# Silu and product of a block one step later, the third convolution tap issued apart, a gate block ahead of branch a

## The chip, the cores and the metric

The kernel runs on one core of a Trainium2 chip. It computes one layer of an encoder trunk on 512 tokens of width 2048, in fp32. The metric is the time of one execution in device microseconds (us), the median of several runs.

The engines in the tables: PE is TensorE (matmuls), PEld its weight loads, DVE is VectorE, ACT is ScalarE, POOL is GpSimd and SP is SyncE, which issues most of the DMAs. Each engine works off its own queue in order.

## The reference, cut to what matters

```python
h = rmsnorm(x, norm_mix[l])
proj = h @ w_in[l]
qa, ka, va, qb, kb, vb, ga, gb = jnp.split(proj, split_points, axis=-1)
...
merged = (jax.nn.sigmoid(ga) * (out_a @ w_branch_a[l])
          + jax.nn.sigmoid(gb) * (out_b @ w_branch_b[l]))
x = x + merged @ w_out[l]

h2 = rmsnorm(x, norm_ffn[l])
u = h2 @ w_up[l]
up = jnp.pad(u, ((0, 0), (1, 1), (0, 0)))
cw = conv_w[l]
u = up[:, :-2] * cw[0] + up[:, 1:-1] * cw[1] + up[:, 2:] * cw[2] + conv_b[l]
gate, val = jnp.split(u, 2, axis=-1)
x = x + (jax.nn.silu(gate) * val) @ w_down[l]
```

`out_a` is a windowed attention with 8 heads, `out_b` a neighbourhood attention with 8 heads. D_FF is 5632, so `w_up` has 11264 columns: 5632 for the gate and 5632 for the value.

## The kernel before

Activations lie transposed, 128 features on the partitions and 512 tokens along the row. Every fp32 product is made of three matmuls in the faster fp32r format: each operand is split into a rounded part (hi) and the rest (lo), the rounding by a cast on ACT and the rest by a subtraction on DVE, and hi·hi, hi·lo and lo·hi are added up in PSUM (L77). So every weight that PE uses passes through ACT and DVE first: L154 and L155 for most stages, L594 and L595 for the up-projection.

**Steps and units.** The layer is a list of steps: attention with its projections, then gate and branch blocks, w_out, 22 up-projection steps, and the down-projection. A step is a sequence of units; the weights of a unit are loaded by SP, split by ACT and DVE two units ahead of PE, and two buffers of each kind hold them, so the split for unit n+2 waits until PE has done unit n. After the matmuls of a unit were issued, `run_queued` takes entries from a queue of postponed work, in the up-projection one entry per unit. In an engine's queue that work stands among the splits in this order.

**Gates and branches.** A block is 512 output columns, four tiles m of 128 by 512. Before: gate blocks 0 and 1 of branch a, then `end_attention` (it closes the memory of attention and opens new pools, with all eight PSUM banks) and the loading and splitting of the eight `out_a` tiles through three scratch tiles (`split_out`), then the four blocks of branch a, then gate blocks 2 and 3. Where the gate came first, `evac_a` multiplies the matmul's result with it; where the branch came first, `evac_a` copies the result (L743) and `gate_after` multiplies later (L736).

**Up-projection.** A step makes 256 gate columns and 256 value columns with seven products in place of eight (a Strassen-like scheme): eight units (i = 0 to 7), each of 7 products with 2 halves with 3 matmuls of 256 columns, 42 in all. `Product.prep` (L594, L595) splits the seven combined weight blocks. Seven of the eight PSUM banks hold the sums; at the step's end `combine` reads them, first by the copy L673 on ACT, and the next step's matmuls take the banks as they come free. The results are two tiles with tag u, 128 by 1024 each: gate and val.

Then the work on them is put into the queue, and is done during the next step: scaling with the norm's row (`scale`, L832, DVE), the convolution over tokens (`conv`), Silu of the gate (L857, ACT), the product (L861, DVE) and the store to `act` in DRAM (L862, POOL). `conv` makes three scaled copies of a tile for the three taps, two ACT instructions each (L840, L842, L843), and adds the outer two to the middle one by two accumulating DMAs that POOL issues (L844, L845); the second waits for the first, as both write the same tile. Tag o (the sum) and tag a (the outer taps) have two buffers each. The queue of a step, by unit of the step in which it runs:

```python
wait, partial(scale, gate), pending_act.pop(),
lambda: held.update(g=conv(gate, 2 * s)), wait, partial(scale, val), silu,
lambda: held.update(v=conv(val, 44 + 2 * s))
```

The first entry runs at unit 7 of the step that made the tiles, the next ones at units 0 to 6 of the following step: scaling of the gate at 0, the product of the tiles of a step earlier at 1, convolution of the gate at 2, scaling of the value at 4, Silu at 5, convolution of the value at 6.

**Into and out of the up-projection.** The pool `w` for the split weights of the up-projection lies where the weight pool `wst` lay, and is opened in `post` of w_out's last block, after its matmuls and evacuations; then two products are split and the last two pairs of h2 formed (`form_pair`). During the last up step, `split_act` loads tiles of `act` back by SP and splits them (L890, L891) for the down-projection, load and split in one.

## Time and profile before

| | |
|---|---|
| median of 3 runs | 2581.73 us (2580.41 to 2588.13) |
| the profiled execution | 2588.31 us |
| its span, first to last instruction | 2586.5 us |
| mean granted clock of TensorE | 0.994 |
| up-projection, from the first to the last of its matmuls | about 1198 to 2104 us |

How to read it: the page gives, for each engine, the time in which it was busy and its share of the span. A list of waits gives who waited for whom, in total, how often and the longest. A timeline row gives start, duration, engine, line of the kernel, operation, output <- input and, in brackets, how long the engine had been idle before and what ended that. A windows row gives for a stretch of the span the busy time of each engine (with the number of instructions), the clock that PE was granted (1.00 is full), the share of the DMA engines that was busy, and what they moved in GB/s. A group row gives line, engine, operation, shapes, number, then busy time and the mean in ns of one, then idle time before them and what ended it. The ends of matmuls are modelled, so PE's idle time is a little rough.

### The profile page before, as it was taken

Reading aid. Unit: us, or ns where it says so; the run is one execution under the profiler, and the core shown is the slowest. Engines: PE = TensorE matmul, PEld = TensorE weight load, DVE = VectorE, ACT = ScalarE, POOL = GpSimd, SP = SyncE. Lnnn points to the kernel's source line nnn. Section 1 sums busy time; section 2 is a strip of 40 time slices with the busy share of each in tenths; the row PEclk is TensorE's granted clock in tenths of the full one; section 3 lists DMA queues with packets and bytes.
Section 4 is the critical chain, followed back from the end, with each engine's and each line's share of the span. In section 5 each row is a group of like instructions: output and inputs, shape, how many; then the busy total and the mean of one; then the engine's idle time right before and its main releaser. Section 6 shows DMA issues by size and latency. Waiting matters only on the chain.

```text
span 2586.5 us, 38229 instructions
## 1 busy us (share of the span) xinstructions
PE 2537.2 (98%) x15016; PEld 2254.9 (87%) x15016; DVE 1517.3 (59%) x2155; ACT 1123.6 (43%) x1617; POOL 206.4 (8%) x248
## 2 busy tenths in 40 slices
PE   9999999999999999999999999999999999999999
PEld 7888888888888888888999999999999988888887
DVE  6565554535454567656777787777778662242222
ACT  5355544432222233335555655566555562132111
POOL 0100000000000000100011111111111110000000
PEclk9999999999999999999999999999999999999999
DMA  5322232327777787854677877777777785464443
GB/s 184 98 83 90 87 96 92 96 90 269 239 260 251 250 278 270 286 188 155 165 200 186 214 198 193 215 192 198 188 185 202 214 252 169 134 214 136 130 126 111
DMA packets 294677, 464.67 MB, mean 180 GB/s; under 512 B 23136, under 2 KB 190688, under 8 KB 294496
## 3 DMA queue, kind: packets, MB, share of 16 engines
q1 hardware_dynamic: 249408, 348.00, 42.6%
q0 software_dynamic: 40480, 105.83, 16.6%
q10 hardware_dynamic: 4608, 8.39, 0.8%
q8 instruction: 117, 1.92, 0.3%
q14 instruction: 64, 0.52, 0.1%
HBM read 347.93 MB, written 68.16 MB: 161 GB/s over the span
## 4 chain that ended last, share of the span: by engine, by line
PE 88%; ACT 5%; DMA 4%; issue 2%; DVE 1%; SPq 0%; POOL 0%; ACTq 0%; POOLq 0%; DVEq 0%
PE mm L77 85%; DMA o<-a 3%; PE tr L77 2%; ACT wh L594 1%; ACT o L840 1%; ACT a L843 1%; ACT a L842 1%; PE tr L476 1%; PE tr L334 0%; DMA f<-in_w_up 0%; DVE wl L595 0%; ACT t L673 0%; DMA f<-sums 0%; DMA s<-act 0%; SPq L74 0%
## 5 line engine op out<-in xcount | busy, mean ns | idle before, releaser
L77 PE MATMUL mm<-s,hi 128*128 128x512 f32 x3712 | 1107.6, 390 | 3.9 <-ACT s L227 2.1
L77 PE MATMUL mm<-s,wh 128*128 128x256 f32 x4928 | 826.3, 281 | 33.6 <-ACT t L673 24.3
L77 PEld LDWEIGHTS mm<-s,hi 128*128 128x128 f32 x3712 | 696.7, 188 | 148.3 <-ACT s L227 2.5
L77 PEld LDWEIGHTS mm<-s,wh 128*128 128x128 f32 x4928 | 712.6, 190 | 38.5 <-ACT t L673 27.8
L155 DVE TENSOR_TENSOR lo<-raw,hi 128x1024 fp32r<-128x1024 f32 (+1 forms) x289 | 352.6, 1220 | 666.9 <-ACT hi L154 648.4
L77 PE MATMUL mm<-s,lo 128*128 128x512 f32 x1856 | 681.9, 390 | 0.0
L154 ACT CAST hi<-raw 128x1024 fp32r<-128x1024 f32 (+1 forms) x289 | 303.4, 1050 | 854.3 <-PE mm L77 792.8
L77 PE MATMUL mm<-s,wl 128*128 128x256 f32 x2464 | 589.9, 280 | 2.3 <-DVE wl L595 2.3
L595 DVE TENSOR_TENSOR wl<-f,wh 128x1024 fp32r<-128x1024 f32 x352 | 372.5, 1087 | 164.0 <-ACT wh L594 152.6
L594 ACT CAST wh<-f 128x1024 fp32r<-128x1024 f32 x352 | 315.2, 939 | 275.7 <-PE mm L77 211.5
L77 PEld LDWEIGHTS mm<-s,wl 128*128 128x128 f32 x2464 | 424.1, 190 | 2.9 <-DVE wl L595 2.9
L77 PEld LDWEIGHTS mm<-s,lo 128*128 128x128 f32 x1856 | 348.6, 188 | 71.5
L77 PE MATMUL mm<-hi,s 128*128 128x512 f32 x896 | 284.8, 394 | 5.7 <-ACT hi L154 5.7
L77 PEld LDWEIGHTS mm<-hi,s 128*128 128x128 f32 x896 | 167.7, 189 | 38.4 <-ACT hi L154 5.7
L77 PE MATMUL mm<-lo,s 128*128 128x512 f32 x448 | 176.2, 394 | 0.0
L573 DVE TENSOR_TENSOR f<-f 128x512 f32<-128x512 f32 x176 | 120.4, 684 | 0.0
L77 PEld LDWEIGHTS mm<-lo,s 128*128 128x128 f32 x448 | 84.4, 188 | 16.7
L580 POOL DMA_DIRECT2D sums<-f x76 | 40.6, 535 | 574.2 <-DVE f L577 455.9
L844 POOL DMA_DIRECT2D o<-a x44 | 52.3, 1189 | 380.7 <-ACT a L842 364.8
L577 DVE TENSOR_TENSOR f<-f 128x256 f32<-128x256 f32 x176 | 74.7, 424 | 5.5
L576 DVE TENSOR_TENSOR f<-f 128x256 f32<-128x256 f32 x176 | 74.6, 424 | 5.3
L840 ACT ACTIVATE o<-u,smalls 128x512 f32<-128x512 f32 x88 | 71.1, 808 | 3.1 <-DVE o L861 0.8
(133 smaller groups left out, 1465.3 us busy)
## 6 DMA issues: line engine op xcount, KB each, us to landing
f<-in_w_up SPq DMA_DIRECT2D x252, 256.0 KB, 3.6
f<-in_w_up SPq DMA_DIRECT2D x428, 128.0 KB, 3.6
raw<-in_w_in SPq DMA_DIRECT2D x103, 512.0 KB, 4.0
raw<-in_w_down SPq DMA_DIRECT2D x88, 512.0 KB, 4.0
o<-a POOLq DMA_DIRECT2D x88, 511.0 KB, 5.5
sums<-f POOLq DMA_DIRECT2D x76, 512.0 KB, 5.3
f<-sums SPq DMA_DIRECT2D x76, 512.0 KB, 5.2
raw<-in_w_in SPq DMA_DIRECT2D x66, 256.0 KB, 3.1
```

The lines of the kernel that those rows point to most:

```text
L77: nc.tensor.matmul(o, l, r, start=start, stop=stop, skip_group_check=True)
L154: nc.scalar.copy(hi[:, c:c + n], self.raw[:, c:c + n])
L155: nc.vector.tensor_tensor(lo[:, c:c + n], self.raw[:, c:c + n], hi[:, c:c + n].bitcast(F32), ALU.subtract)
L476: nc.tensor.transpose(b[:, (j - j0) * P:(j - j0 + 1) * P], pr[j][:, off:off + P], ident)
L573: keep(nc.vector.tensor_tensor(f[:, 3:5], f[:, 2::-2], f[:, 6].unsqueeze(1).to_broadcast([P, 2, 256]), ALU.add))
L576: keep(nc.vector.tensor_tensor(f[:, 5], f[:, 4], f[:, 2], ALU.add))
L577: keep(nc.vector.tensor_tensor(f[:, 6], f[:, 5], f[:, 1], ALU.add))
L580: nc.gpsimd.dma_start(self.kept, self.f[:, 3:])
L594: keep(nc.scalar.copy(hi, f))
L595: keep(nc.vector.tensor_tensor(lo, f, hi.bitcast(F32), ALU.subtract))
L840: keep(nc.scalar.activation(o[:, m], u[:, m], AF.Identity, bias=cb[:, i:i + 1], scale=cw[:, i, 1:2]))
L844: nc.gpsimd.dma_start(o[:, :, 1:], before[:, :, :S - 1], accum_op=ALU.add)
```

## The change

- `up`: Silu and product of a step's tiles are queued with the next step's work. At unit 0 Silu of the tiles of a step earlier runs ahead of the gate's scaling; the product stays at unit 1; the gate's convolution stays at unit 2; the value's scaling moves to unit 3.
- `conv` becomes a class: `middle` issues the middle and first tap and the first accumulating DMA, `last` the third tap and the second DMA. For the gate both run at unit 2; for the value `middle` runs at unit 4 and `last` at unit 6.
- `split_act` is parted: `load_act` issues the DMAs, and the split follows one unit later and is kept in program order.
- The third gate block of branch a is moved in front of branch a; the eight `out_a` tiles are loaded at its start into their own slots and split at its last four units. `evac_a` multiplies in three of four blocks.
- The pool `w` is opened at the last unit of w_out, and one product is split there. Its tiles have one buffer per parity of the product in place of two buffers per tag.

```diff
@@ prep_to
-            if isinstance(u, Product) and "w" not in ffn:
+            if isinstance(u, Product) and u.first > ffn.get("limit", -1):
                 break
@@ Product.prep
-                    ffn["w"].tile([P, n * 256 + 32], F32R, tag=half + tag, name="w" + half, bufs=2)[
-                        :, at:at + n * 256].rearrange("p (f n) -> p f n", f=n)
+                    ffn["w"].tile(
+                        [P, n * 256 + 32], F32R, tag=f"{half}{tag}{self.first % 2}",
+                        name="w" + half, bufs=1)[:, at:at + n * 256].rearrange(
+                            "p (f n) -> p f n", f=n)
@@ gates and branches
-            tag = {2: "u", 3: "o"}.get(m // 4) if store is sg else None
+            tag = ({2: "u", 3: "o"} if store is sg else {2: "a"}).get(m // 4)
...
-        if m < 8:
+        if m < 12:
             nc.vector.tensor_tensor(ra[m], ps, ra[m], ALU.mult)
         else:
-            ra[m] = slot_of("a" if m < 12 else None)
+            ra[m] = slot()
             nc.scalar.copy(ra[m], ps)
...
+    def load_parts(src):
+
+        hi, lo = slot(F32R), slot(F32R)
+        dma(lo.bitcast(F32), src)
+        return hi, lo
+
+    def split_parts(hi, lo):
+        raw = lo.bitcast(F32)
+        nc.scalar.copy(hi, raw)
+        nc.vector.tensor_tensor(lo, raw, hi.bitcast(F32), ALU.subtract)
...
-    def before_a():
+    def load_a():
         end_attention()
-        split_out(oa, out_a)
-
+        oa.extend(load_parts(o) for o in out_a)
+
+    def before_gate(kb):
+        if kb >= 4:
+            for parts in oa[2 * kb - 8:2 * kb - 6]:
+                split_parts(*parts)
+
+    gates(C_GA, 8, gate_first(ra), pre=load_a, before=before_gate)
     for blk in range(4):
-        branch(w_branch_a, blk * 4, oa, evac_a, pre=before_a if blk == 0 else None)
-    for blk in range(2, 4):
-        gates(C_GA, blk * 4, gate_after)
+        branch(w_branch_a, blk * 4, oa, evac_a)
+    gates(C_GA, 12, gate_after)
@@ project_out, before and post
+            if n == 3 and kb == 7:
+                wst_ctx.close()
+                ffn["w"] = ctx.enter_context(tc.tile_pool(name="w", bufs=2, reuse_waits="tile"))
+                ffn["limit"] = at["use"] + 1
...
             if n == 3:
-                wst_ctx.close()
-                ffn["w"] = ctx.enter_context(tc.tile_pool(name="w", bufs=2, reuse_waits="tile"))
+                ffn["limit"] = len(units)
                 prep_to(at["use"] + 1)
@@ the convolution
+        def middle(self):
+            u, self.o, first = self.u, quad("o"), quad("a")
+            for m in range(2):
+                i = self.idx + m
+                keep(nc.scalar.activation(
+                    self.o[:, m], u[:, m], AF.Identity, bias=cb[:, i:i + 1], scale=cw[:, i, 1:2]))
+                keep(nc.scalar.activation(first[:, m], u[:, m], AF.Copy, scale=cw[:, i, 0:1]))
+            nc.gpsimd.dma_start(self.o[:, :, 1:], first[:, :, :S - 1], accum_op=ALU.add)
+
+        def last(self):
+            third = quad("a")
+            for m in range(2):
+                keep(nc.scalar.activation(
+                    third[:, m], self.u[:, m], AF.Copy, scale=cw[:, self.idx + m, 2:3]))
+            nc.gpsimd.dma_start(self.o[:, :, :S - 1], third[:, :, 1:], accum_op=ALU.add)
@@ up
+            before, after = unfinished.popleft(), unfinished.popleft()
             queue.extend((
-                wait, partial(scale, gate), pending_act.pop(),
-                lambda: held.update(g=conv(gate, 2 * s)), wait, partial(scale, val), silu,
-                lambda: held.update(v=conv(val, 44 + 2 * s))))
-            pending_act.append(out_part)
+                wait, lambda: (before(), scale(gate)), after, lambda: (g.middle(), g.last()),
+                partial(scale, val), v.middle, wait, v.last))
+            unfinished.extend((silu, out_part))
...
             if s == pairs_ff - 1 and i >= 1:
-                split_act(0, i - 1)
+                load_act(0, i - 1)
+                split_act(0, i - 2)
@@ down
             if part == n == 0:
-                if kb + 7 < len(parts[0]):
-                    split_act(0, kb + 7)
+                load_act(0, kb + 7)
+                split_act(0, kb + 6)
                 if kb == 9:
-                    queue.append(pending_act.pop())
+                    queue.extend(unfinished)
             if part == 0 and n == 3:
-                split_act(1, kb)
+                load_act(1, kb)
+                split_act(1, kb - 1)
+            if part == 1 and n == 0 and kb == 0:
+                split_act(1, len(parts[0]) - 1)
```

More of the change, by code (lines that the diff above doesn't have):

```diff
@@ L749, in evac_b @@
         merged[m] = split(r)
+    def load_parts(src):
[6 more added lines that the diff above has]
+        nc.vector.tensor_tensor(lo, raw, hi.bitcast(F32), ALU.subtract)
     def split_out(dst, src):
         for o in src:
-            t = scratch()
-            dma(t, o)
-            dst.append(split(t))
+            dst.append(load_parts(o))
+            split_parts(*dst[-1])
     for blk in range(2):
         gates(C_GA, blk * 4, gate_first(ra))
-    def before_a():
+    def load_a():
         end_attention()
-        split_out(oa, out_a)
+        oa.extend(load_parts(o) for o in out_a)
[4 more added lines that the diff above has]
+    gates(C_GA, 8, gate_first(ra), pre=load_a, before=before_gate)
     for blk in range(4):
-        branch(w_branch_a, blk * 4, oa, evac_a, pre=before_a if blk == 0 else None)
-    for blk in range(2, 4):
-        gates(C_GA, blk * 4, gate_after)
+        branch(w_branch_a, blk * 4, oa, evac_a)
+    gates(C_GA, 12, gate_after)
     def before_b(kb):
@@ L833, in scale, with __init__ @@
             u, u, rows["f"].unsqueeze(1).to_broadcast([P, 2, S]), ALU.mult))
-    def conv(u, idx):
-        o, before, after = quad("o"), quad("a"), quad("a")
-        for m in range(2):
-            i = idx + m
-            keep(nc.scalar.activation(
-                o[:, m], u[:, m], AF.Identity, bias=cb[:, i:i + 1], scale=cw[:, i, 1:2]))
-            keep(nc.scalar.activation(before[:, m], u[:, m], AF.Copy, scale=cw[:, i, 0:1]))
-            keep(nc.scalar.activation(after[:, m], u[:, m], AF.Copy, scale=cw[:, i, 2:3]))
-        nc.gpsimd.dma_start(o[:, :, 1:], before[:, :, :S - 1], accum_op=ALU.add)
-        nc.gpsimd.dma_start(o[:, :, :S - 1], after[:, :, 1:], accum_op=ALU.add)
-        return o
+    class Conv:
+        def __init__(self, u, idx):
+            self.u, self.idx = u, idx
+        def middle(self):
[12 more added lines that the diff above has]
+            nc.gpsimd.dma_start(self.o[:, :, :S - 1], third[:, :, 1:], accum_op=ALU.add)
@@ L848, in trunk_kernel @@
     parts = [range(pairs_ff // 2), range(pairs_ff // 2, pairs_ff)]
     acts = [[], []]
-    pending_act = [lambda: None]
+    wait = lambda: None
+    unfinished = deque([wait, wait])
     def up(s):
         def evac(gate, val):
-            held = {}
+            g, v = Conv(gate, 2 * s), Conv(val, 44 + 2 * s)
             def silu():
-                keep(nc.scalar.activation(held["g"], held["g"], AF.Silu))
+                keep(nc.scalar.activation(g.o, g.o, AF.Silu))
             def out_part():
-                g, v = held["g"], held["v"]
-                keep(nc.vector.tensor_tensor(v, g, v, ALU.mult))
-                nc.gpsimd.dma_start(act[s], v)
-            wait = lambda: None
+                keep(nc.vector.tensor_tensor(v.o, g.o, v.o, ALU.mult))
+                nc.gpsimd.dma_start(act[s], v.o)
+            before, after = unfinished.popleft(), unfinished.popleft()
@@ L882, in up, with load_act @@
                  kept=range(8) if s in (0, pairs_ff - 1) else (2, 3, 7))
+    def load_act(part, n):
+        for i in range(2 * (0 <= n < len(parts[part]))):
+            acts[part].append(load_parts(act[parts[part][n]][:, i]))
     def split_act(part, n):
-        for i in range(2 * (n < len(parts[part]))):
-            hi, lo = slot(F32R), slot(F32R)
+        for hi, lo in acts[part][2 * max(n, 0):2 * n + 2]:
             raw = lo.bitcast(F32)
-            dma(raw, act[parts[part][n]][:, i])
-            nc.scalar.copy(hi, raw)
-            nc.vector.tensor_tensor(lo, raw, hi.bitcast(F32), ALU.subtract)
-            acts[part].append((hi, lo))
+            keep(nc.scalar.copy(hi, raw))
+            keep(nc.vector.tensor_tensor(lo, raw, hi.bitcast(F32), ALU.subtract))
     def down(part, n):
```

## The prediction

> **What bounds the kernel now.** I read the page first, for the load of each engine.

> ```profile
> span 2586.5 us, 38229 instructions
> PE 2537.2 (98%) x15016; PEld 2254.9 (87%) x15016; DVE 1517.3 (59%) x2155; ACT 1123.6 (43%) x1617; POOL 206.4 (8%) x248
> ```

> TensorE (PE) is the bound, and the change neither adds nor removes a matmul: it can win only where PE stands still or runs at a lower clock. So the second view is the list of PE's waits (us in total, times, longest us).

> ```profile
> PE mm L77 <- ACT t L673: 25.1, 18, 3.1
> PE mm L77 <- ACT wh L594: 9.3, 6, 3.9
> PE mm L77 <- ACT hi L154: 6.7, 2, 5.7
> PE mm L77 <- DVE wl L595: 2.3, 3, 0.8
> PE mm L77 <- ACT s L227: 2.1, 1, 2.1
> ```

> The largest, 18 times, is on the copy at L673, the first read of the finished PSUM banks of an up-projection step; there are 22 such steps. The third view places the waits: busy time of the engines by stretch (start:end, length, busy PE, PEld, DVE, ACT, POOL, then granted clock, DMA share, GB/s).

> ```profile
> 579.00:589.00 10.00, 7.94 (x29) 6.13 (x28) 6.18 (x9) 5.66 (x10) 0.00 (x0) 0.83 0.29 100
> 579.00:600.00 21.00, 17.95 (x71) 14.10 (x70) 10.58 (x14) 9.00 (x14) 0.00 (x0) 0.92 0.62 215
> 1187.00:1212.00 25.00, 20.93 (x142) 18.86 (x141) 19.91 (x39) 15.77 (x30) 3.98 (x5) 1.00 0.33 116
> 1212.00:2050.00 838.00, 814.34 (x6955) 810.25 (x6955) 641.09 (x810) 493.63 (x645) 104.34 (x97) 0.99 0.75 196
> 1319.00:1329.00 10.00, 7.30 (x49) 7.18 (x48) 7.18 (x11) 6.46 (x10) 2.41 (x2) 0.83 0.56 124
> 1401.00:1411.00 10.00, 8.25 (x58) 8.05 (x57) 7.19 (x11) 6.45 (x10) 2.39 (x2) 0.83 0.57 124
> 1561.00:1571.00 10.00, 7.60 (x51) 7.40 (x51) 7.18 (x11) 6.50 (x10) 2.38 (x2) 0.83 0.56 122
> 1841.00:1855.00 14.00, 9.49 (x65) 8.88 (x65) 8.38 (x12) 10.76 (x15) 2.10 (x2) 0.88 0.40 98
> 1886.00:1900.00 14.00, 9.93 (x58) 9.32 (x57) 8.52 (x12) 10.75 (x15) 2.42 (x2) 0.76 0.47 127
> 2050.00:2106.00 56.00, 46.99 (x361) 45.62 (x360) 35.16 (x42) 37.71 (x56) 6.55 (x6) 0.94 0.81 243
> ```

> Length less PE busy is idle time; length times (1 less clock) is what the lower clock costs. Four places lose time. A, start of branch a: 21 − 17.95 = 3.05 idle, 10 × 0.17 = 1.7 clock: 4.75 us. B, start of the up-projection: 25 − 20.93 = 4.07. C, boundaries between up steps: 838 − 814.34 = 23.66 idle, and 1.7 + 1.7 + 1.7 + 1.68 + 3.36 = 10.1 clock in the five short rows: 33.8. D, the last up step and the start of down: 9.01 idle, 56 × 0.06 = 3.36 clock: 12.4. Together **55.0 us** is the most that can be won.

> What makes a boundary late is seen on ScalarE's (ACT's) timeline before one of them, then PE's, then POOL's.

> ```profile
> 1677.89 1.06 ACT L857 ACTIVATE o<-o 128x1024 f32<-128x1024 f32 x1 [3.30 <-DMA o<-a]
> 1678.86 1.76 ACT L594 CAST wh<-f 128x1024 fp32r<-128x1024 f32 x2
> 1680.53 0.81 ACT L840 ACTIVATE o<-u,smalls 128x512 f32<-128x512 f32 x1
> 1681.25 0.71 ACT L842 ACTIVATE a<-u,smalls 128x512 f32<-128x512 f32 x1
> ...
> 1684.40 0.56 ACT L673 COPY t<-mm 128x512 f32<-128x512 f32 x1
> ...
> 1685.02 0.51 PE L77 MATMUL mm<-s,wh 128*128 128x256 f32 x2 [1.01 <-ACT t L673]
> ...
> 1665.12 1.17 POOL L844 DMA_DIRECT2D o<-a  x1 [2.80 <-ACT a L842]
> 1671.47 1.19 POOL L845 DMA_DIRECT2D o<-a  x1 [5.17 <-ACT wh L594]
> ...
> ACT o L857 <- DMA o<-a: 72.7, 20, 7.3
> ```

> The gate block's convolution issues two accumulating DMAs; the second waits for the first. Silu (L857) needs both, so ACT stands 3.30 us (20 of 22 times, 72.7 us in all). Behind Silu in ACT's queue are two casts, the six scalings of the value block's convolution, and only then the copy, 1684.40 − 1677.89 = 6.51 us after Silu began. PE had ended its step at 1685.02 − 1.01 = 1684.01.

> **The change part by part.** *Silu and product one step later (C).* Silu keeps its 1.06 us on ACT and the product its place, but Silu now runs at unit 0 of the following step, when its DMAs have landed; nothing then waits at unit 5. Removed from the path: the 3.30 us wait. The value block's six scalings (1680.53 to 1684.40, 3.9 us) are split: four at unit 4, two at unit 6. So between the last casts and the copy stand two scalings, 1.4 us, where six stood. In the step shown they would begin at the same 1680.5 at the latest, and the copy at 1681.9, 2.1 us before PE is done instead of 0.4 us after.

> The largest idle time at a boundary is 14 − 9.49 = 4.5 us. There is a **new wait**: the value's third-tap product takes one of two buffers with tag a, which the gate's second accumulating DMA must have left; that is the landing for which Silu waited. It comes some 0.6 us earlier, since the gate's first DMA no longer stands behind one third-tap scaling (0.71). Even where it binds, the copy follows it by 1.4 us, not 6.51: 5.1 + 0.6 = 5.7 us sooner, more than 4.5. Behind the waiting scaling ACT holds the copy and the casts of the next weights, and PE waits for those. The value's first DMA is now queued on POOL behind the gate's second one and not behind Silu; its buffer is freed by the gate's first landing, before unit 4 unless that is slow. The product on DVE comes two units after the value's last landing, as before, so I cost it at nothing; without that cover it would hold DVE's casts.

> I leave 1.6 us in C (gain 32.2): what the two busiest boundaries may keep. Bounds: 0 and 33.8.

> *Load apart from split, and the last step (D).*

> ```profile
> ACT s L890 <- DMA s<-act: 24.5, 16, 3.8
> ```

> The activations read back are loaded one unit before they are split. The DMAs are the same in number and order on SP, so SP's queue gets no longer; of the 24.5 us of ACT waits those inside the last up step go. They and Silu's wait make D's stalls. In that step ACT still gets up to 14 extra casts, and a unit's lead is about the landing time, so I leave 2.5 of 12.4: gain 9.9 (0 to 12.4).

> *The gate block ahead of branch a (A).*

> ```profile
> 566.57 21.59 SPq L74 DMA_DIRECT2D t<-out_a  x8
> 580.31 0.69 DVE L712 TENSOR_TENSOR s<-mm,row 128x512 f32<-128x512 f32 x1 [0.67 <-PE mm L77]
> L743 ACT COPY a<-mm 128x512 f32<-128x512 f32 x4 | 2.3, 586 | 2.1 <-PE mm L77 2.1
> ```

> Now eight loads share three scratch tiles and take SP 21.59 us, and branch a waits for the splits. In the change the eight go out together into their own slots, and a gate block of 192 matmuls lies ahead of their first use, over 40 us (the row at 579 has 71 in 17.95 us, part of them at the lower clock). It hides the loads and the splits, two at each of its last four units; without it the 4.75 us come back. On SP the loads go behind weights that are already asked for. Four copies (2.3 us) and four products on DVE fall away, off PE's path: nothing. What is late next: the new PSUM pool opens at the same place, and its first bank may wait for the last gate product, 580.31 + 0.69 = 581.00, after PE ended at 580.3. I leave 0.8: gain 3.9 (0 to 4.75).

> *The first up weights cast before w_out ends (B).*

> ```profile
> 1196.64 3.45 ACT L594 CAST wh<-f 128x1024 fp32r<-128x1024 f32 x4
> 1197.72 1.95 PE L77 MATMUL mm<-s,wh 128*128 128x256 f32 x14 [3.00 <-ACT wh L594]
> 1199.65 2.95 DVE L595 TENSOR_TENSOR wl<-f,wh 128x768 fp32r<-128x768 f32 x3
> 1209.16 3.22 DVE L595 TENSOR_TENSOR wl<-f,wh 128x1024 fp32r<-128x1024 f32 x3
> ```

> One product's casts move to w_out's last unit, which removes the 3.00 us. But the third product's wl at 1209.16 stands behind DVE's work on h2. PE comes 3.0 us earlier, DVE is rid of only about 2.2 us (two wl, 1.2 and 0.95), so the later stall grows from 1.07 by 0.8 to about 1.9. Gain 2.1. Bounds: 4.07, and −1.7 if that one idle time brings a lower clock such as in A.

> **Sum:** 32.2 + 9.9 + 3.9 + 2.1 = 48.1. The profiled execution took 2588.31 us, so 2540.2. It lies 6.6 above the median of 2581.73; taken off the median the same gain gives 2533.6. I cannot tell whether the 6.6 us are stalls that the change would remove, and take the middle, **2537**.

> [...] In the trace the clock falls behind idle times of 1.75 us (10 − 8.25 in the row at 1401). [...]

> **The rivals.**
> *The low-clock stretches stay,* because something other than the gaps makes them. The trace shows each right behind a gap and speaks against it. Price: 1.7 + 10.1 + 3.36 = 15.2, less gain: about 2552. [...]

> *Another matmul spacing.* The weight tiles change address (tag by parity). The trace has two speeds without any wait:

> ```profile
> 1484.00:1498.00 14.00, 14.00 (x119) 14.00 (x120) 12.05 (x14) 5.96 (x8) 1.46 (x2) 1.00 0.71 154
> 1498.00:1521.00 23.00, 23.00 (x205) 23.00 (x204) 19.50 (x27) 16.80 (x22) 2.97 (x3) 1.00 0.87 241
> ```

> 14/119 is 117.6 ns, 23/205 is 112.2, an estimated 5 ns for each of 7392 matmuls, and the slow part is some 14 of 38.8 us of a step. 7392 is 22 steps of 8 units of 42, and 38.8 is (78 − 0.43)/2 from the next row. If the addresses set it, all slow costs 7392 × 0.64 × 5 ns = 23 us: 2560; all fast wins 13: 2524.

> *DVE or ACT keeps a part of the boundaries.*

> ```profile
> 1483.00:1561.00 78.00, 77.57 (x675) 77.36 (x674) 61.93 (x78) 46.73 (x62) 10.71 (x10) 1.00 0.78 203
> ```

> Here two steps run almost without a gap, DVE at 61.93/78 = 79%, ACT at 60%: room enough on average, but if bursts keep 1 us at each of 21 boundaries, 2558.

> *Slower: the third-tap buffer.*

> ```profile
> 2080.38 1.18 POOL L844 DMA_DIRECT2D o<-a  x1 [3.69 <-ACT a L842]
> 2091.09 1.20 POOL L845 DMA_DIRECT2D o<-a  x1 [9.53 <-ACT s L890]
> DMA to landing us min/median/max: 4.8/5.5/9.3
> ```

> The gate's two DMAs, one behind the other, begin about 1664.5. The last scalings and the copy need 2.0 us before PE's end at 1684.0, so the chain may take 17.5 us; in the step shown it took 12.8 (1665.12 to 1677.89). If more DMAs in flight made each landing as slow as the 10.7 us from 2080.38 to 2091.09, the chain were 21.4: 3.9 late and 1.7 of clock at each of 21 boundaries, 118 where the sum has 1.6: about 2653. From some 19 us of chain the kernel is slower than before. Against it: the maximum in C is 9.3, and no DMA is added.

> *The change doesn't do what it says:* the compiled order leaves Silu where it was, and C and most of D stay: 2537 + 32 + 8 = 2577.

> **How the numbers follow.** Forecast (2528 to 2547) 0.57; fast spacing 0.05; slow spacing 0.10; clock stays 0.05; bursts keep a part 0.15; order unchanged 0.03; slower 0.05. The range 2522 to 2562 takes in all but the last two. What can be told from no change is 0.3%, 7.7 us: faster 0.92, same 0.03, slower 0.05.

> **What would show it.** Right: no wait of Silu on the DMA; the waits on L673's copy nearly gone; clock 1.00 from 1212 to the end of up; up steps of about 38.6 us. A wrong: a wait at the gate block's start above 1 us. B wrong: a stall at the third product above 2 us. Wrong in C: ACT waiting at the third tap for o<-a, or DVE's casts ending PE's waits. The spacing would show in the matmuls per us of a stretch without waits.

## The result, and the profile after

The changed kernel takes 2525.77 us (median of 4 runs, 2524.26 to 2526.30), the kernel before 2584.26 in the same series (2580.41 to 2588.13). The ratio is 0.9773, 95% interval 0.9755 to 0.9791. The profiled executions took 2526.16 and 2588.31 us, so they differ by 62.15. The page after, its span and the load of the engines:

```profile
span 2524.4 us, 38263 instructions
...
PE 2510.1 (99%) x15016; PEld 2233.5 (88%) x15016; DVE 1514.3 (60%) x2155; ACT 1120.3 (44%) x1613; POOL 205.8 (8%) x248
```

PE has the same 15016 matmuls, and its busy time is 27.1 us shorter, so it is not idle time alone that went. The list of all PE waits after (us in total, times, longest):

```profile
PE mm L77 <- ACT hi L154: 5.6, 1, 5.6
PE mm L77 <- ACT wh L596: 2.5, 1, 2.5
PE mm L77 <- DVE wl L597: 1.1, 2, 0.8
PE mm L77 <- DVE s L714: 0.9, 1, 0.9
PE mm L77 <- ACT t L675: 0.3, 1, 0.3
```

The first is the kernel's start. The copy of the finished banks (L673, now L675) held PE 18 times for 25.1 us, and now once for 0.3. Windows after, at places A, B, C and D of the prediction (the third is 20 whole up steps, the second to the twenty-first), and the same 20 steps before:

```profile
579.00:600.00 21.00, 20.12 (x89) 16.40 (x88) 12.50 (x18) 9.79 (x15) 0.73 (x1) 1.00 0.61 196
1183.00:1203.00 20.00, 17.52 (x104) 15.84 (x103) 14.76 (x28) 11.22 (x23) 2.16 (x4) 0.91 0.38 131
1235.94:2001.42 765.48, 765.48 (x6723) 765.48 (x6721) 624.98 (x792) 486.44 (x636) 105.53 (x98) 1.00 0.79 208
1990.00:2045.00 55.00, 53.95 (x454) 52.82 (x453) 39.23 (x46) 40.15 (x58) 8.94 (x8) 1.00 1.01 291
```

```profile
1240.70:2051.45 810.75, 787.09 (x6723) 783.00 (x6721) 625.85 (x791) 482.53 (x632) 104.34 (x97) 0.99 0.75 197
```

In the 20 steps PE no longer stands still at all, and the same matmuls also keep it busy 21.6 us less. A, B and D keep 0.88, 2.48 and 1.05 us of idle time, and B alone a lower clock, 0.91.

Both kernels issue equally many matmuls, so the time from the start of one matmul to the start of another of the same number can be set side by side. That shows where the 62.15 us came from:

| stretch, by number of the matmul | before | after | gain |
|---|---|---|---|
| A: 2500 to 3000 | 113.8 | 109.7 | 4.1 |
| B: 5000 to the end of the first up step | 158.56 | 157.65 | 0.9 |
| C: up steps 2 to 21 | 810.75 | 765.48 | 45.3 |
| D: last up step and 60 matmuls of down | 65.7 | 53.6 | 12.1 |

The four make 62.4; the kernel's start gives 0.2 of it back.

ScalarE's rows at one boundary after (the twelfth, the one the prediction shows of before), with PE's first matmul of the next step:

```profile
1651.92 1.78 ACT L596 CAST wh<-f 128x1024 fp32r<-128x1024 f32 x2 [2.15 <-PE mm L77]
1653.61 1.33 ACT L873 ACTIVATE a<-u,smalls 128x512 f32<-128x512 f32 x2
1654.85 0.56 ACT L675 COPY t<-mm 128x512 f32<-128x512 f32 x1
...
1657.02 0.40 PE L77 MATMUL mm<-s,wh 128*128 128x256 f32 x2
```

Between the last casts and the copy stand two scalings, and the copy begins 2.2 us before PE begins the next step. In the kernel before, PE's rows at this boundary are these, and the gap that ended at 1685.02 comes behind them:

```profile
1683.14 0.40 PE L77 MATMUL mm<-s,wh 128*128 128x256 f32 x2
1683.38 0.28 PE L77 MATMUL mm<-s,wl 128*128 128x256 f32 x1
1683.50 0.40 PE L77 MATMUL mm<-s,wh 128*128 128x256 f32 x2
1683.73 0.28 PE L77 MATMUL mm<-s,wl 128*128 128x256 f32 x1
```

Counted by number, the matmul at 1683.14 is the first of the next step. So the copy (1684.40) began 1.3 us after PE had begun that step, and the six matmuls before the gap are the step's first product, which goes into the eighth bank. In the kernel before, 17 of the 18 waits on this copy stand behind six such matmuls.

### The profile page after: what moved, and what is told of

The parts are those of the page before. It is cut to its first block, busy times and chain, and to the rows that moved or that the text cites. A ratio compares the mean times of both kernels' runs of the same rounds, so it can differ in the third digit from the quotient of the medians.

```text
span 2524.4 us, 38263 instructions
## 1 busy us (share of the span) xinstructions
PE 2510.1 (99%) x15016; PEld 2233.5 (88%) x15016; DVE 1514.3 (60%) x2155; ACT 1120.3 (44%) x1613; POOL 205.8 (8%) x248
## 4 chain that ended last, share of the span: by engine, by line
PE 97%; DMA 2%; ACT 1%; DVE 0%; issue 0%; SPq 0%; ACTq 0%; DVEq 0%; POOLq 0%
PE mm L77 93%; PE tr L77 2%; PE tr L476 1%; DMA o<-a 1%; DMA s<-act 0%; PE tr L334 0%; ACT wh L596 0%; DMA f<-sums 0%; DVE wl L597 0%; PE tr L383 0%; DMA f<-in_w_up 0%; DMA raw<-in_w_in 0%; ACT s L632 0%; ACT t L248 0%; SPq L74 0%
## 5 line engine op out<-in xcount | busy, mean ns | idle before, releaser
L77 PE MATMUL mm<-s,hi 128*128 128x512 f32 x3712 | 1106.2, 390 | 0.9 <-DVE s L714 0.9
L77 PEld LDWEIGHTS mm<-s,hi 128*128 128x128 f32 x3712 | 695.9, 188 | 144.0 <-ACT s L715 1.3
L77 PE MATMUL mm<-s,wh 128*128 128x256 f32 x4928 | 807.0, 277 | 2.8 <-ACT wh L596 2.5
L77 PEld LDWEIGHTS mm<-s,wh 128*128 128x128 f32 x4928 | 701.0, 188 | 3.5 <-ACT wh L596 2.9
L154 ACT CAST hi<-raw 128x1024 fp32r<-128x1024 f32 (+1 forms) x289 | 303.5, 1050 | 879.5 <-PE mm L77 810.6
L77 PE MATMUL mm<-s,lo 128*128 128x512 f32 x1856 | 681.8, 390 | 0.0
L77 PE MATMUL mm<-s,wl 128*128 128x256 f32 x2464 | 583.6, 277 | 1.1 <-DVE wl L597 1.1
L77 PEld LDWEIGHTS mm<-s,wl 128*128 128x128 f32 x2464 | 419.0, 188 | 1.5 <-DVE wl L597 1.5
L77 PEld LDWEIGHTS mm<-s,lo 128*128 128x128 f32 x1856 | 348.5, 188 | 71.5
L77 PE MATMUL mm<-hi,s 128*128 128x512 f32 x896 | 285.0, 394 | 5.6 <-ACT hi L154 5.6
L77 PEld LDWEIGHTS mm<-hi,s 128*128 128x128 f32 x896 | 167.8, 189 | 38.4 <-ACT hi L154 5.6
L77 PE MATMUL mm<-lo,s 128*128 128x512 f32 x448 | 176.3, 395 | 0.0
L77 PEld LDWEIGHTS mm<-lo,s 128*128 128x128 f32 x448 | 84.6, 189 | 16.8
```

Of the source, the lines that this page charges most:

```text
L77: nc.tensor.matmul(o, l, r, start=start, stop=stop, skip_group_check=True)
L154: nc.scalar.copy(hi[:, c:c + n], self.raw[:, c:c + n])
```

## The experiments

All changes are against the changed kernel unless the text says otherwise. "Slow" matmuls are those of the up-projection's 7392 whose start follows the one before by 116 to 121 ns (118 on average; the others 113.4). The times are medians; the kernel before, run beside them, had medians of 2578.8 to 2580.6. The changed kernel was not run again beside them, so a small difference rests on its four runs (2524.26 to 2526.30) and on the profiles.

**1. The places of the weight tiles, put back.**

```diff
-                        [P, n * 256 + 32], F32R, tag=f"{half}{tag}{self.first % 2}",
-                        name="w" + half, bufs=1)
+                        [P, n * 256 + 32], F32R, tag=half + tag,
+                        name="w" + half, bufs=2)
```

> The changed kernel with the weight tiles of the up-projection taken as before (one tag, two buffers, instead of a tag by parity). Of the changed kernel's 7392 matmuls of 256 columns in the up-projection 924 start some 118 ns after the one before, and 6420 some 113.4; in the kernel before it was 2205 and 4709. Theory 'addresses': the places of the tiles set the spacing. Then about 2200 matmuls are slow again, and the time is some 9 us longer than the changed kernel's 2526, about 2535, with PE's waits as short as there (under 5 us in all). Rival 'order': the spacing follows the stalls and the order of the work. Then about 920 are slow and the time is 2524 to 2528.

2535.36 us (2534.89 to 2537.57), 2603 slow matmuls. Its window of the 20 steps:

```profile
1236.08:2011.11 775.03, 775.03 (x6723) 775.03 (x6721) 625.37 (x793) 488.09 (x638) 105.53 (x98) 1.00 0.78 206
```

No idle time and full clock, as in the changed kernel, yet 9.55 us longer with equally many matmuls. So the places change the spacing, 2603 slow matmuls against the changed kernel's 924; the rival falls.

**2. The new places alone, in the kernel before.** The opposite edit.

> The kernel before with the tag by parity alone. Theory 'addresses': some 920 slow matmuls instead of 2205, the time some 9 us below that of the kernel before, about 2575, the waits on the copy of the finished banks unchanged (some 25 us in 18). Rival 'order': about 2200 slow matmuls, no difference that can be measured (within 3 us of the kernel before).

2580.71 us (2572.39 to 2588.84) where the kernel before took 2579.38: ratio 1.0007, interval 0.9987 to 1.0026. 790 slow matmuls, as the theory said, but not the time that it said. The 20 steps:

```profile
1246.29:2051.65 805.36, 779.29 (x6722) 775.28 (x6720) 624.54 (x791) 481.22 (x631) 104.35 (x97) 0.99 0.76 198
```

PE is busy 7.8 us less than before, and its idle time grows from 23.66 to 26.07 us: PE reaches the boundary sooner and waits there longer, since the chain on ScalarE that ends at the copy has not become shorter. That gives back 2.4 us, and the 20 steps are 5.4 us shorter. This profile loses 5.1 us again near 923 us, in the gate blocks, which the edit does not touch: two waits of 0.4 and 2.4 us and a stretch at half clock. What took the gain in the other runs is open.

**3. All weights at one offset.** The first unit of each step lies 28 elements into its tile, the others 16.

```diff
-                at = 28 if self.turn else 16
+                at = 16
```

> The changed kernel with the weights of the first unit of each step at the same offset in their tile as all the others (16 and not 28 elements). Theory 'addresses': the 924 slow matmuls, which are those of the first unit, become fast: 4.3 us less, about 2522, under 100 slow ones. Rival 'order': it is the first unit's place in the step (first use of the banks, the reads of the finished ones beside it) that makes them slow: 924 remain, 2526. A third case, in which the other offset is what ends a slow state: slow matmuls in other units too, up to 7392 x 4.6 ns = 34 us more, to 2556.

2521.66 us (2520.44 to 2522.40), below the changed kernel's runs, 28 slow matmuls. Its 20 steps:

```profile
1235.68:1997.28 761.60, 761.60 (x6722) 761.60 (x6721) 625.37 (x793) 487.82 (x638) 105.52 (x98) 1.00 0.80 209
```

761.60 us for 6720 matmuls of the up-projection is 113.3 ns each: hardly any is slow any more.

**4. Old places and one offset.** Edits 1 and 3 together.

> The changed kernel with the weight tiles taken as before (2603 slow matmuls, 2535.4 us) and all weights at the common offset. Theory 'a state': the first unit's other offset starts the slow spacing, and the old places of the tiles only let it last longer, two to four units; without that offset there is none: under 100 slow, 2521 to 2524. Rival 'the place alone': the tiles of units 1 to 3 are slow where they lie; some 1700 slow ones remain, 2529 to 2532.

2521.28 us (2520.62 to 2524.49), 156 slow, the 20 steps again 761.60. So the old places are not slow by themselves: 156 slow matmuls, against 2603 when the first unit has the other offset. In these runs the slow spacing comes with the unit at that offset, and how long it lasts changes with the places of the tiles. Whether the value of 28 does it or only the difference from the other units was not tried. Counted along PE's order in groups of 42, a unit's number of matmuls, 63, 72, 65 and 63% of the first four groups of a step are slow with the old places (edit 1), 66, 30 and 2% with the new ones. What in the chip this is no run shows.

**5. The whole queue of the up-projection as before** (the third tap beside the others, Silu at unit 5).

```diff
-                partial(scale, val), v.middle, wait, v.last))
-            unfinished.extend((silu, out_part))
+                wait, partial(scale, val), silu, lambda: (v.middle(), v.last())))
+            unfinished.extend((wait, out_part))
```

> The changed kernel with the up-projection's queue as before: Silu and product in their own step, the third tap beside the other two; all else as changed. Theory: the boundaries between steps were lost to Silu's wait and to what stands behind it. Then the waits on the copy of the finished banks come back, 20 to 25 us in some 18 waits, with 7 to 10 us at the lower clock, and the time is 2554 to 2562. Rival: other parts (the loads apart from the splits, the new places of the weight tiles) removed a good part of the boundaries too; then it is 2530 to 2550. If the spacing follows the stalls, about 1200 more slow matmuls come with them, some 9 us on top.

2572.93 us (2564.68 to 2589.11): 47 us more than the changed kernel, more than the 28 to 36 that the theory said, without additional slow matmuls (838). The profiled execution took 2568.93. ScalarE's and PE's waits:

```profile
ACT o L887 <- DMA o<-a: 71.8, 20, 7.5
...
PE mm L77 <- ACT t L675: 22.4, 14, 3.1
```

The 20 steps take 795.26 us in it, 29.8 more, and the last step with the start of down 66.5, 12.9 more: the queue as before makes D's loss too, which the expectation had left out.

**6 and 7. One half of it each.** Silu at its old unit, the third tap apart:

```diff
-                partial(scale, val), v.middle, wait, v.last))
-            unfinished.extend((silu, out_part))
+                partial(scale, val), v.middle, silu, v.last))
+            unfinished.extend((wait, out_part))
```

> The changed kernel with Silu put back into its own step, ahead of the value block's third tap; the third tap stays apart from the other two, and the product stays in the next step. Against the changed kernel the whole queue as before costs 43 to 47 us. Theory 'Silu's wait': ScalarE waits for the landing at this place whatever stands behind it; most comes back: 2555 to 2570. Rival 'what stands behind Silu': in the kernel before four scalings more stood between Silu and the copy, 2.5 us; the boundaries lost at most 4.5 us and mostly under 2, so with two scalings the copy is late at a few boundaries only: 2530 to 2545.

2531.50 us (2531.11 to 2531.65). And Silu in the next step, the three taps together (at unit 6, the queue's last entry):

```diff
-                partial(scale, val), v.middle, wait, v.last))
+                wait, partial(scale, val), wait, lambda: (v.middle(), v.last())))
```

> The changed kernel with Silu and product in the next step, but the value block's three taps together at the step's last unit, as before. Theory 'Silu's wait': without it the six scalings (3.9 us) start up to 4.4 us earlier than in the kernel before (3.3 of waiting and 1.06 of Silu), and the copy comes before TensorE's end: 2526 to 2532. Rival 'the six scalings': they are issued behind the last casts and hold the copy wherever Silu is: the waits on the copy come back at most of the boundaries, 2545 to 2570.

2526.82 us (2525.25 to 2528.92). Undoing both costs 47 us, undoing one 5.7 or 1.1. In the sixth kernel ScalarE still waits at Silu. The wait and the same boundary read as follows; the copy begins 2.3 us before PE begins the next step (1660.06):

```profile
ACT o L887 <- DMA o<-a: 27.0, 18, 4.2
```

```profile
1653.50 1.07 ACT L887 ACTIVATE o<-o 128x1024 f32<-128x1024 f32 x1 [0.78 <-DMA o<-a]
1654.87 1.78 ACT L596 CAST wh<-f 128x1024 fp32r<-128x1024 f32 x2 [0.30 <-DVE f L573]
1656.56 1.33 ACT L873 ACTIVATE a<-u,smalls 128x512 f32<-128x512 f32 x2
1657.80 0.57 ACT L675 COPY t<-mm 128x512 f32<-128x512 f32 x1
```

What counts is when the copy starts against PE's end, taken here as the start of the step's last matmul plus one spacing of 0.113 us. Over all 22 boundaries of a profile, from the rows of the copies and of PE, the means are:

| kernel | copy starts, us after PE's end |
|---|---|
| before | 1.36 |
| queue as before (5) | 1.36 |
| taps together (7) | -0.07 |
| Silu at its old unit (6) | -1.75 |
| changed | -2.13 |

The wait and the work behind it stand in series and are held against one limit. Either half of the edit brings the copy under it; the other half then adds little but slack. In the seventh kernel 18 of 22 copies start within 0.02 us of PE's end, and almost nothing is lost: PE still has the six matmuls for the eighth bank, 0.68 us, and the copy takes 0.56, so an estimated 0.1 us after PE's end is still in time. In the sixth expectation the rival came true, in the seventh the theory: Silu's wait costs most boundaries only together with the four scalings behind it.

**8. Load and split together again** (last up step and down; the splits are also no longer kept in program order).

```diff
-                split_act(0, i - 2)
+                split_act(0, i - 1)
...
-                split_act(0, kb + 6)
+                split_act(0, kb + 7)
```

> The changed kernel with load and split of the activations together, as before, in the last up step and in the down-projection. Theory: the loads made a part of what the last up step lost: ScalarE waits for landings inside that step again, TensorE idles 3 to 8 us there and beyond, 2530 to 2536. Rival: Silu's wait made all of it; then ScalarE waits for the loads, but TensorE does not: 2524 to 2528.

2532.43 us (2529.84 to 2540.40), in the theory's range. The waits of ScalarE and of PE:

```profile
ACT s L921 <- DMA s<-act: 29.0, 19, 6.1
...
PE mm L77 <- ACT wh L596: 6.0, 3, 2.5
```

ScalarE waits 29.0 us for the loads (3.9 in the changed kernel), and two more waits of PE come from casts behind them. Of D's 12.1 us 3.9 come back in this profile, which is the fastest of the four runs; the median run loses 6.7.

**9. The pool of the up weights opened behind w_out again.**

```diff
-            if n == 3 and kb == 7:
-                wst_ctx.close()
-                ffn["w"] = ctx.enter_context(tc.tile_pool(name="w", bufs=2, reuse_waits="tile"))
-                ffn["limit"] = at["use"] + 1
...
+                wst_ctx.close()
+                ffn["w"] = ctx.enter_context(tc.tile_pool(name="w", bufs=2, reuse_waits="tile"))
                 ffn["limit"] = len(units)
```

> The changed kernel with the pool of the up weights opened behind w_out, as before. Theory: the compiled order of ScalarE is the same with and without this edit, the first cast stands behind the same instructions of the evacuation; no difference: 2524 to 2528, the first wait of the up-projection 2.5 us. Rival, as predicted: the early pool saves 3.0 us and gives back 0.9: 2528 to 2530, first wait 3.0 us.

2527.15 us (2524.27 to 2528.11), which does not tell it from the changed kernel. The first wait of the up-projection is 3.0 us against 2.5, as the rival said, so the theory was wrong in saying that ScalarE's order is the same. The edit moves the first cast ahead of one square, as the rows of this kernel and then of the changed one show:

```profile
1192.28 0.63 ACT L248 ACTIVATE t<-s 128x512 f32<-128x512 f32 x1
1192.81 3.44 ACT L596 CAST wh<-f 128x1024 fp32r<-128x1024 f32 x4
```

```profile
1191.97 0.39 ACT L632 CAST s<-a 128x256 fp32r<-128x256 f32 x1
1192.27 1.77 ACT L596 CAST wh<-f 128x1024 fp32r<-128x1024 f32 x2
1193.95 0.62 ACT L248 ACTIVATE t<-s 128x512 f32<-128x512 f32 x1
```

In this profile 10.24 us at half clock follow the wait, against 3.41 in the changed kernel, and stretch B is 2.5 us longer. So what the early opening is worth depends on the clock as well, and one profile does not settle it.

**10. The casts really ahead of w_out's evacuation.**

```diff
-            nc.scalar.activation(one, src, AF.Square)
+            op = nc.scalar.activation(one, src, AF.Square)
+            if name == "f" and k >= 12:
+                keep(op)
...
-            nc.scalar.activation(scaled[j][:, i], x2[m], AF.Copy, scale=gffn[:, m:m + 1])
+            op = nc.scalar.activation(scaled[j][:, i], x2[m], AF.Copy, scale=gffn[:, m:m + 1])
+            if j >= 6:
+                keep(op)
```

> The changed kernel with four squares and four scalings of w_out's last evacuation kept behind the first product's casts on ScalarE; no work is added or left out. In the changed kernel the first cast of the up-projection still began 1.4 us after TensorE had ended w_out, behind seven instructions of that evacuation, though its weights had landed 25 us earlier; TensorE waited 2.48 us and then ran 3.4 us at half clock (1.7 us). Theory 'order on ScalarE': the cast begins near 1182, the wait falls under 0.5 us and the lower clock with it: 4.2 us less, 2521 to 2523. Rival 'VectorE': the lower halves still stand behind the evacuation's sums on VectorE, and the wait turns into one on them of about the same length: 2524 to 2527. A later wait may also grow, for the transformed activations of the last two units, which are now formed later: up to 3 us more, 2528.

2529.60 us (2528.69 to 2530.20), slower than the changed kernel. The first cast now begins at 1180.31 us and PE's first wait is 0.24, but another one has come:

```profile
PE mm L265 <- DVE t L264: 5.0, 3, 3.5
```

The row factor's four matmuls begin after 84 up matmuls in PE's rows, 210 in the changed kernel (the 88 and 214 of the expectation count four other matmuls of the row factor too), and VectorE's operands for them are not ready there.

**11. The same, with these matmuls at their old place and all weights at one offset.** `newest` holds the last matmul traced for PE, here that of the fifth unit.

```diff
-            nc.tensor.matmul(b[:, t * P:(t + 1) * P], ones, dg, start=True, stop=True)
+            with tc.issue_after(newest[0].ins) if name == "f" else nullcontext():
+                nc.tensor.matmul(b[:, t * P:(t + 1) * P], ones, dg, start=True, stop=True)
```

> Three edits on the changed kernel: the first unit's weights at the common offset (alone 2521.7), the evacuation's squares and scalings kept behind the first casts (alone 2529.6, since the row factor's four matmuls were then placed after 88 matmuls of the up-projection instead of 214, and TensorE waited 5.0 us for their operands and ran 6.8 us at half clock), and these four matmuls queued behind the fifth unit, 214 as before. Theory: TensorE's wait at the start of the up-projection (2.5 us, and 1.7 us of lower clock) is gone without a new one: 2517 to 2519. Rival: the operands of the four matmuls, or the activations of the last two units, are late at the old place too: 2520 to 2526.

2526.83 us (2525.66 to 2529.43), 5.2 more than edit 3 alone. PE's wait and what ScalarE does before it:

```profile
PE mm L79 <- ACT wh L601: 6.6, 1, 6.6
```

```profile
1206.98 1.32 ACT L637 CAST s<-t 128x256 fp32r<-128x256 f32 x4 [1.69 <-DVE t L633]
1208.20 0.40 ACT L637 CAST s<-a 128x256 fp32r<-128x256 f32 x1
1208.51 3.46 ACT L601 CAST wh<-f 128x1024 fp32r<-128x1024 f32 x4
```

Now the third product's casts stand behind the forming of h2's last pairs, and PE waits 6.6 us. Twice the wait at B was removed and came back longer a few us later. Which order of this work would be shorter is open.

**12. Branch a ahead of the third gate block again,** with the eight loads through three scratch tiles, which undoes A.

```diff
-    gates(C_GA, 8, gate_first(ra), pre=load_a, before=before_gate)
     for blk in range(4):
-        branch(w_branch_a, blk * 4, oa, evac_a)
-    gates(C_GA, 12, gate_after)
+        branch(w_branch_a, blk * 4, oa, evac_a, pre=before_a if blk == 0 else None)
+    for blk in range(2, 4):
+        gates(C_GA, blk * 4, gate_after)
```

> The changed kernel with branch a ahead of the third gate block, its eight loads through three scratch tiles, as before; all else as changed. Theory: the start of branch a loses again what the kernel before lost there, two waits of 3.05 us together and 1.7 us of lower clock, against 0.88 us in the changed kernel: 3.9 us more, 2529 to 2531. Rival: the loads are late for another reason than their three tiles and only part comes back: 2526 to 2528.

2530.16 us (2529.44 to 2532.57), 4.4 more and in the theory's range. PE's first wait of the kernel before at this place is there again:

```profile
PE mm L77 <- ACT s L227: 2.1, 1, 2.1
```

## Why the prediction was right, and where it was not

2537 was forecast and 2525.77 measured, inside the range of 2522 to 2562 and just below the likeliest case's own (2528 to 2547). By its steps, against the profiled pair:

- **A** (gain 3.9, keeps 0.8): 4.1, keeps 0.88. Undone, it costs 4.4. Right in size; that the late loads are the cause fits the wait that comes back, but the three tiles and the place of the loads were not undone apart.
- **B** (gain 2.1): 0.9. The step that failed is "One product's casts move to w_out's last unit, which removes the 3.00 us". The edit allows the casts there, but ScalarE's queue had them only one square earlier, and the wait is still 2.48 us with 1.7 of lower clock. The later stall, put at 1.9, is 0.3. An edit of the program's order was taken for an order of the queue.
- **C** (gain 32.2, keeps 1.6): 45.3. The 23.66 us of idle time went whole. Experiment 1 puts 9.55 of the gain down to the spacing, which was not in this term, so 35.7 are left for idle time and clock, 1.9 more than the 33.8 counted as all that could be won; where these 1.9 sit is open. The mechanism was the one named, the wait and the scalings behind it; that either half of the edit would have done nearly all was not seen, and both were credited. One reading was wrong: PE did not end its step at 1684.01: it began the next one at 1683.14, and by 1684.01 that step's first product was done. Against 1683.14 the copy forecast for 1681.9 lies 1.2 us ahead, and 2.2 were measured, mainly because the last casts, no longer behind Silu, begin 5.1 us ahead of the step's end and not 4.3. The forecast of C does not hang on this, since PE stands still only when that first product is done.
- **D** (gain 9.9, keeps 2.5): 12.1 of 12.4. What was left for ScalarE's extra casts was not needed. Experiments 5 and 8 show both causes named, the old queue with Silu (12.9 when undone) and the loads (3.9).
- **The sum** went by a cap of 55.0, "the most that can be won". That was no cap: it holds idle time and clock, not PE's own pace. The matmul spacing stood among the rivals as an alternative to the forecast, "all fast wins 13: 2524", with 0.05. It came beside the forecast: new places 9.6 us, one offset for all another 4.1, together 13.7 against the estimated 13. The mis-sized term is this one, put at nothing in the sum. Without the new places, in experiment 1, the time is 2535.36, 1.6 below the forecast; that it comes so close has luck in it. Between the profiled runs of the kernel before and of experiment 1 (2534.89) the gain is 53.4, not 48.1, and the middle taken as the base hides 3.2 of the difference.
- **The base.** 2537 took the middle between the profiled 2588.31 and the median; the median of the four runs in this series is 2584.26, so the gain in medians is 58.5, not 62.2. The longest series of the kernel before, 19 runs beside the experiments, has a median of 2579.38 and a range of 2569.32 to 2588.65: the profiled 2588.31 is one of its slowest executions, and against that median the gain is 53.6.
- **The other rivals.** The low clock went with the gaps, and one low stretch is left, 3.41 us at clock 0.50 behind B's wait: the rival "the low-clock stretches stay" falls. Bursts on VectorE or ScalarE hold no boundary. The third tap's buffer became a wait, as named, but a short one:

```profile
ACT a L867 <- DMA o<-a: 4.1, 4, 1.8
ACT a L873 <- DMA o<-a: 3.7, 3, 3.1
```

A landing within the up steps took 6.1 us at the median (5.5 before) and 10.2 at most, not 10.7 each time, and only one of these waits reached PE: 3.1 us of ScalarE at the boundary to the last step, of which 0.29 was left for PE.

## What to carry to other kernels

Work that stands in series ahead of a limit is no sum of gains: measure how late its end is against the point where the waiting engine runs out of work, and expect little from the second edit once the first has brought it under. A faster engine that arrives earlier at the same wait gives a part of its gain back (2.4 of 7.8 us in experiment 2), so idle time and pace are two terms, and both belong in the sum. Whether an edit moved an instruction is read from the queue's rows, not from the program.

## What the runs showed of the hardware

**The half-clock stretches lie on a grid of 3.413 us.** In all 14 profiles the half-clock stretches, but for one at each span's end, are 3.413 us long or two or three times that, on a grid of that length. In the kernel before, the first begins at 582.24 us and the others 217, 241, 288, 371, 384, 432 and 441 times 3.4133 us later. Windows on its grid:

```profile
1401.43:1404.85 3.42, 1.67 (x14) 1.47 (x13) 1.54 (x3) 3.42 (x7) 1.20 (x1) 1.00 0.55 159
1404.85:1408.26 3.41, 3.41 (x18) 3.41 (x17) 2.52 (x3) 2.60 (x3) 0.00 (x0) 0.50 0.81 147
1763.25:1766.66 3.41, 1.74 (x15) 1.54 (x14) 1.71 (x4) 3.41 (x8) 1.20 (x1) 1.00 0.51 154
1766.66:1770.07 3.41, 3.41 (x31) 3.41 (x30) 2.33 (x3) 2.71 (x4) 0.00 (x0) 1.00 0.85 156
```

```profile
1188.94:1192.35 3.41, 2.76 (x13) 1.94 (x11) 3.19 (x7) 3.29 (x7) 1.62 (x3) 1.00 0.38 154
1192.35:1195.77 3.42, 1.60 (x14) 1.60 (x14) 3.42 (x8) 3.42 (x6) 0.54 (x1) 1.00 0.38 153
1195.77:1199.18 3.41, 3.41 (x32) 3.41 (x31) 3.41 (x5) 3.41 (x9) 0.00 (x0) 1.00 0.27 77
```

The runs of the kernel before spread over 20 us (2569.32 to 2588.65 in one series, granted clock 0.991 to 0.996), those of the changed one over 2 (granted clock 0.999 in each); where the spread comes from was not tried.

**The matmuls' spacing changed with the offset of the weights.** 128 x 256 matmuls with equal work start 113.3 or 118 ns apart. Of the up-projection's 7392, 924 are slow in the changed kernel and 2603 with the old places (experiment 1); with one offset for all weights 28 with the new places (experiment 3) and 156 with the old ones (experiment 4).
